# One token tile at a time across the boundary between two layers, partly in plain fp32, and adaLN column sums without GpSimd

## The chip, the core and the metric

The kernel runs on one core of a Trainium2 chip. The metric is the device time of one execution in microseconds (us), the median of several runs. TensorE's granted clock has two levels in these traces, 2.4 GHz (shown as 1.00) and 1.2 GHz (shown as 0.50).

## The reference

Two layers, one after the other, on 256 tokens of width 2048. All is fp32. Cut to what matters here:

```
mod = c @ w_ada + b_ada                      # (2048) @ (2048 x 6144)
shift, scale, gate = split(mod, 3)
u    = layer_norm(x) * (1 + scale) + shift
proj = u @ w_in                              # c_q, c_kv, k_rope, g_a, qkv_b, ... merge_logit
... three attention branches (latent, forgetting, stick-breaking), each gated by silu ...
merged = sum over branches of sigmoid(merge_logit) * (y_n @ w_branch[n])
out  = merged @ w_out                        # (256 x 2048) @ (2048 x 2048)
x    = layer_norm(ALPHA * x + gate * out, ln_g, ln_b)
```

The first product of the second layer needs the rows that the first layer's last layer norm gives, normalised once more and modulated. So the boundary between the layers is a chain: output projection, residual, norm over a row, norm again, transpose, modulate, first product.

## The kernel before

**Tiles.** The 256 tokens are two tiles of 128 (`t` = 0, 1); the width is 16 blocks of 128 (`k`). Activations are the stationary operand of TensorE, weights are the moving one, 512 columns in a matmul, summed in a PSUM bank of 128x512.

**Products in three terms.** Each fp32 operand is split into a rounded part `hi` in the format fp32r and a remainder `lo`; a product is hi·hi + hi·lo + lo·hi, three fp32r matmuls of 128x512 into one bank (`Gemm.multiply`, lines 271 to 273). The weights are split as they arrive: `weight_unit` (line 212) loads 2 k-blocks x 1024 columns (1 MB) on the SP queue into one of four `raw` buffers, ScalarE makes `whi` (line 225), VectorE makes `wlo` (line 227); there are four buffers of each. One pair of 128x1024 feeds 12 matmuls (2 token tiles x 2 halves x 3 terms).

**Order of the work.** The tile framework orders the instructions of each engine at build time: of those that its model takes to be ready, the earliest in the program goes first. The order on each engine is then fixed; on the chip an instruction that waits holds back all behind it on its engine. `tc.issue_after(ins)` keeps instructions behind `ins` on its engine.

**adaLN sums.** c @ w_ada is done in thirds (shift, scale, gate), beside other work: a list `background` is worked off, some pieces per weight unit (`credit`), and emptied by `drain_background`. VectorE sums c·w_ada over 16 steps into `ada_acc` (128 x 2048, line 290), so that a sum over the 128 partitions is left. GpSimd does that with a partition_all_reduce of 128x2048 (line 317). For shift and scale VectorE then masks the result with the identity (line 329) and reduces it (line 332) to 128x16; the gate's row goes to DRAM (line 320). This path serves four of the six thirds: layer 0's gate and all three of layer 1. Layer 0's shift and scale are made by `ada_pieces` (line 549).

**The boundary.** Layer 0's output projection runs as two products of 1024 columns (`cc` = 0, 1; line 849), each for both token tiles; the second finishes its banks one after the other (`stagger`). `evac_out` (lines 844 to 847) multiplies a bank by the gate, adds the residual and takes bn_stats: three VectorE instructions per bank. When all banks of a tile are there, lines 859 to 870 normalise its row: an aggregate, rsqrt (nine instructions on 128x1, lines 179 to 187), four 128x512 instructions on line 864 and four on line 868. `normalise_row` (lines 350 to 359) squares the row on ScalarE for the variance, takes another rsqrt and writes `xn`, half on VectorE and half on ScalarE. `modulate` (line 361) transposes two k-blocks of both tiles on TensorE (line 365) and makes `uhi` and `ulo`. Then `first` (line 526), the first product of layer 1 (columns 0 to 1023 of w_in, all 16 k-blocks, both tiles), can begin.

Of the kernel before, what the change touches and what calls it, by code (L numbers as in the profile page):

```python
# [9 lines left out]
F32 = mybir.dt.float32  # L10
# [27 lines left out]
C0 = GB0 + BW  # L38
M0 = C0 + 4 * BW


@with_exitstack
def trunk(
# [81 lines left out]
    nc.gpsimd.memset(m_mla[0:64, P + 64:], NEG)  # L125
    rst = const.tile([P, 3 * P], F32, name="rst")
# [85 lines left out]
    def weight_unit(parts, width, u):  # L212
        raw = wpool.tile([P, 2, CH], F32, tag="raw", name="raw")
        o = 0
        for src, c0, w in parts:
# [4 lines left out]
            o += w  # L220
        pairs = []
        for j in range(2):
            hi = wpool.tile([P, CH], F32R, tag="whi", name="whi")
            lo = wpool.tile([P, CH], F32R, tag="wlo", name="wlo")
            nc.scalar.activation(hi[:, :width], raw[:, j, :width], AF.Copy)  # L225
            with tc.issue_after(state["first"].ins) if "first" in state else nullcontext():
                state["dve"] = nc.vector.tensor_tensor(  # L227
                    out=lo[:, :width], in0=raw[:, j, :width], in1=hi[:, :width].bitcast(F32), op=ALU.subtract
                )
            pairs.append((hi, lo))  # L230
        return pairs

    class Gemm:
# [9 lines left out]
        def unit(self, u):  # L243
            if u == 0:
                for t in range(NT):
                    for h in range(len(self.cuts)):
                        self.banks[t, h] = acc_tile()
            pairs = weight_unit(self.parts, self.width, u)
# [16 lines left out]
        def multiply(self, t, h, k, pair):  # L265
# [4 lines left out]
            ah, al = ahi[:, k, t * P:(t + 1) * P], alo[:, k, t * P:(t + 1) * P]  # L270
            nc.tensor.matmul(ps, ah, hi[:, o:o + w], start=k == 0, stop=False)  # L271
            nc.tensor.matmul(ps, ah, lo[:, o:o + w], start=False, stop=False)  # L272
            nc.tensor.matmul(ps, al, hi[:, o:o + w], start=False, stop=k == self.nk - 1)  # L273
# [7 lines left out]
    def gemm(*args):  # L281
        Gemm(*args).run()
# [18 lines left out]

    mods = [const.tile([P, 2, KT], F32, name=f"mod{l}") for l in range(DEPTH)]
    gates = {}

    def queue_ada(l, third, tag="ada"):
# [16 lines left out]
        def done():  # L322
# [583 lines left out]
```

## Time and profile before

| what | value |
|---|---|
| median of 3 runs | 2176.76 us (2174.96 to 2179.47) |
| the profiled execution | 2176.92 us, its span 2175.2 us |
| mean granted clock of TensorE | 0.985 |
| TensorE matmul busy | 2071.8 us, 95% of the span |
| VectorE busy | 1455.5 us, 67% |
| ScalarE busy | 984.4 us, 45% |
| GpSimd busy | 66.5 us, 3% |
| moved by DMA | 483 MB, 222 GB/s |

The span runs from the first to the last instruction; the execution's own time is 1.7 us longer. A busy share is an average over stages. Matmuls are pipelined and their ends are modelled, so what a matmul costs in a stream is read from the distance between starts. One fp32 matmul that isn't fp32r is recorded as two.

### The profile page before, as it was taken

What the parts mean: (1) busy time and instruction counts of PE and PEld (TensorE: products, weight loads), DVE (VectorE), ACT (ScalarE), POOL (GpSimd) and SP (SyncE); (2) the same over time, 40 slices, a digit from 0 to 9 for tenths busy, and PEclk for the clock granted to TensorE, in tenths of its full rate; (3) what the DMA queues carried; (4) which work ended last, traced back from release to release, by engine and by line L of the source; (5) the groups of instructions that cost most, each with busy time, mean ns of one, the idle gap of its engine ahead of it and who ended that gap; (6) DMA issues with size and microseconds to landing.
All of it is one profiled execution on the core that took longest, in us unless ns stands there. A gap on an engine that the chain in (4) does not pass through costs nothing. (4 is left out here: it accounts for less than half of the span.)

```text
span 2175.2 us, 24840 instructions
## 1 busy us (share of the span) xinstructions
PE 2071.8 (95%) x9606; PEld 1700.4 (78%) x9606; DVE 1455.5 (67%) x1951; ACT 984.4 (45%) x1257; POOL 66.5 (3%) x79
## 2 busy tenths in 40 slices
PE   4999999999999999999969999999989999999996
PEld 2877888887788878787848888888868888878885
DVE  6898855777558777888587755555575544466466
ACT  4535644444453445634354644444434444464441
POOL 0000000002000020002000000000020000000000
PEclk8999999999999999999979999999999999999998
DMA  8996635787548867786635646666654555556652
GB/s 312 344 332 242 194 117 183 281 309 270 195 145 313 316 232 261 292 320 222 201 135 169 232 136 232 232 230 225 233 178 161 191 193 188 194 180 209 190 200 97
DMA packets 138133, 483.14 MB, mean 222 GB/s; under 512 B 14736, under 2 KB 18976, under 8 KB 127520
## 3 DMA queue, kind: packets, MB, share of 16 engines
q1 hardware_dynamic: 133296, 464.69, 61.6%
q0 software_dynamic: 2432, 16.81, 2.0%
q8 instruction: 75, 1.23, 0.2%
q10 hardware_dynamic: 2288, 0.07, 0.1%
q14 instruction: 42, 0.34, 0.0%
HBM read 477.31 MB, written 4.23 MB: 221 GB/s over the span
## 5 line engine op out<-in xcount | busy, mean ns | idle before, releaser
L227 DVE TENSOR_TENSOR wlo<-raw,whi 128x1024 fp32r<-128x1024 f32 (+2 forms) x648 | 813.0, 1261 | 559.6 <-ACT whi L225 559.3
L225 ACT ACTIVATE whi<-raw 128x1024 fp32r<-128x1024 f32 (+2 forms) x648 | 677.5, 1051 | 826.9 <-PE acc L273 784.1
L272 PE MATMUL acc<-wlo,uhi 128*128 128x512 f32 (+1 forms) x1856 | 733.3, 395 | 11.4 <-DVE wlo L227 11.3
L271 PE MATMUL acc<-whi,uhi 128*128 128x512 f32 (+1 forms) x1856 | 728.4, 394 | 4.0 <-ACT whi L225 3.9
L273 PE MATMUL acc<-whi,ulo 128*128 128x512 f32 (+1 forms) x1856 | 727.9, 392 | 0.0
L272 PEld LDWEIGHTS acc<-wlo,uhi 128*128 128x128 f32 x1856 | 351.5, 189 | 80.3 <-DVE wlo L227 13.3
L271 PEld LDWEIGHTS acc<-whi,uhi 128*128 128x128 f32 x1856 | 350.0, 189 | 73.0 <-ACT whi L225 4.3
L273 PEld LDWEIGHTS acc<-whi,ulo 128*128 128x128 f32 x1856 | 351.1, 189 | 67.1
L272 PE MATMUL acc<-wlo,yhi 128*128 128x512 f32 x384 | 149.5, 389 | 2.0 <-DVE wlo L227 2.0
L273 PE MATMUL acc<-whi,ylo 128*128 128x512 f32 x384 | 149.4, 389 | 0.0
L271 PE MATMUL acc<-whi,yhi 128*128 128x512 f32 x384 | 149.4, 389 | 0.0
L290 DVE SCALAR_TENSOR_TENSOR ada_acc<-raw_ada,c_sb,ada_acc 128x2048 f32<-128x2048 f32 x60 | 140.7, 2345 | 0.1
L271 PE MATMUL acc<-whi,mhi 128*128 128x512 f32 x256 | 99.7, 391 | 2.0 <-ACT mhi L191 2.0
L273 PE MATMUL acc<-whi,mlo 128*128 128x512 f32 x256 | 100.5, 392 | 0.0
L272 PE MATMUL acc<-wlo,mhi 128*128 128x512 f32 x256 | 100.0, 391 | 0.0
L317 POOL PARTITION_ALL_REDUCE ada_acc<-ada_acc x4 | 49.9, 12472 | 1248.7 <-DVE ada_acc L290 736.9
L272 PEld LDWEIGHTS acc<-wlo,yhi 128*128 128x128 f32 x384 | 72.1, 188 | 17.5 <-DVE wlo L227 2.5
L273 PEld LDWEIGHTS acc<-whi,ylo 128*128 128x128 f32 x384 | 72.1, 188 | 14.9
L271 PEld LDWEIGHTS acc<-whi,yhi 128*128 128x128 f32 x384 | 72.1, 188 | 14.9
L610 PE MATMUL acc<-wlo,uhi 128*128 128x512 f32 (+1 forms) x192 | 73.6, 386 | 6.4 <-DVE wlo L601 6.4
L609 PE MATMUL acc<-whi,uhi 128*128 128x512 f32 (+1 forms) x192 | 72.1, 384 | 3.7 <-DVE sum_b L615 2.2
L600 ACT ACTIVATE whi<-raw_g 128x1024 fp32r<-128x1024 f32 (+1 forms) x48 | 46.3, 1002 | 59.1 <-DMA raw_g<-in_w_in_dram 53.9
(232 smaller groups left out, 1790.1 us busy)
## 6 DMA issues: line engine op xcount, KB each, us to landing
raw<-in_w_in_dram SPq DMA_DIRECT2D x224, 1024.0 KB, 5.0
raw_ada<-in_w_ada_dram SPq DMA_DIRECT2D x64, 1024.0 KB, 4.8
raw<-in_w_branch_dram SPq DMA_DIRECT2D x48, 1024.0 KB, 5.6
raw_s<-in_w_ada_dram SPq DMA_DIRECT2D x64, 512.0 KB, 5.0
raw<-in_w_out_dram SPq DMA_DIRECT2D x32, 1024.0 KB, 5.5
raw_g<-in_w_in_dram SPq DMA_DIRECT2D x16, 1024.0 KB, 5.8
raw<-in_w_in_dram SPq DMA_DIRECT2D x8, 832.0 KB, 4.4
raw<-in_w_uq_dram SPq DMA_DIRECT2D x8, 768.0 KB, 4.8
```

Of the source, the lines that this page charges most:

```text
L225: nc.scalar.activation(hi[:, :width], raw[:, j, :width], AF.Copy)
L227: state["dve"] = nc.vector.tensor_tensor(out=lo[:, :width], in0=raw[:, j, :width], in1=hi[:, :width].bitcast(F32), op=ALU.subtract)
L271: nc.tensor.matmul(ps, ah, hi[:, o:o + w], start=k == 0, stop=False)
L272: nc.tensor.matmul(ps, ah, lo[:, o:o + w], start=False, stop=False)
L273: nc.tensor.matmul(ps, al, hi[:, o:o + w], start=False, stop=k == self.nk - 1)
L290: nc.vector.scalar_tensor_tensor(out=acc, in0=raw, scalar=col, in1=acc, op0=ALU.mult, op1=ALU.add)
L317: nc.gpsimd.partition_all_reduce(acc, acc, P, bass_isa.ReduceOp.add)
L600: nc.scalar.activation(hi, raw[:, 2 * j:2 * j + 2, :w], AF.Copy)
L609: nc.tensor.matmul(ps, ah, hi, start=j == 0, stop=False)
L610: nc.tensor.matmul(ps, ah, lo, start=False, stop=False)
```

## The change

It touches three things.

1. **adaLN sums.** The partition_all_reduce is gone. `fold` lets VectorE transpose the 128x2048 sums in blocks of 32x32 and reduce them to 128x64; `done` adds the four groups of 32 partitions with a small matmul against `sel32` and adds the bias in four instructions. The gate's row is transposed and sent to DRAM on ScalarE's queue with its bias in it, so the load and the add of `bg` before the output projection go.
2. **Layer 0's output projection, last 1024 columns.** Columns 1024 to 1535 for both tiles; then columns 1536 to 2047 for tile 0 in three terms, then for tile 1 in plain fp32 (`m_last` by the unsplit weights `held`). Each tile's norms stand in the program right behind its columns.
3. **Layer 1's first product.** Its first 8 k-blocks (`PLAIN`) run in plain fp32, tile 0 and then tile 1 (`start_tile`), from unsplit weights; the other 8 in three terms as before. `hi` and `lo` of the first 8 blocks are still made, for the products that follow. Transposes ahead of a split now go by one token tile and four k-blocks.

```diff
-        def total():
-            acc = ada["acc"]
-            nc.gpsimd.partition_all_reduce(acc, acc, P, bass_isa.ReduceOp.add)
-            if third == 2:
-                gates[l] = dram.tile([1, D], F32, name=f"gate{l}")
-                nc.gpsimd.dma_start(out=gates[l], in_=acc[:1])
+        def fold():
+            acc = ada["acc"]
+            turned = wpool.tile([P, 2, CH], F32, tag="raw", name="turned").rearrange("p j n -> p (j n)")
+            part = tmp.tile([P, SEQ], F32, tag="um", name="part", bufs=2)[:, :D // 32]
+            with tc.issue_after(state["dve"].ins):
+                nc.vector.transpose(turned, acc)
+                nc.vector.tensor_reduce(
+                    out=part, in_=turned.rearrange("p (b j) -> p b j", j=32), axis=mybir.AxisListType.X, op=ALU.add)
+            ada["part"] = part
         def done():
-            acc = ada["acc"]
-            with tc.issue_after(state["dve"].ins):
-                diagonal(l, third, acc)
+            ps = att_tile()
+            nc.tensor.matmul(ps[:, :D // 32], sel32, ada["part"], start=True, stop=True)
+            sums = gsum if third == 2 else mods[l][:, third]
+            for j in range(4):
+                q = slice(32 * j, 32 * j + 32)
+                nc.vector.tensor_tensor(out=sums[q], in0=ps[q, j:D // 32:4], in1=bT[l][q, third], op=ALU.add)
             if third == 2:
+                nc.tensor.transpose(ps[:KT, 2 * P:3 * P], gsum, ident)
+                rows = tmp.tile([P, SEQ], F32, tag="um", name="rows", bufs=2)[:KT, :P]
+                nc.vector.tensor_copy(out=rows, in_=ps[:KT, 2 * P:3 * P])
+                gates[l] = dram.tile([1, D], F32, name=f"gate{l}")
+                nc.scalar.dma_start(out=gates[l].rearrange("o (k p) -> (o k) p", p=P), in_=rows)
-        background.append(total)
-        if third < 2:
-            background.extend([lambda: None, lambda: None, done])
+        background.append(fold)
+        background.extend([lambda: None, done])
...
+    def modulated(l, xt_n, k0, um):
+        ps = att_tile().rearrange("p (k s) -> p k s", k=4)
+        for j in range(4):
+            nc.tensor.transpose(ps[:, j], xt_n[:, (k0 + j) * P:(k0 + j + 1) * P], ident)
+        for j in range(4):
+            k = k0 + j
+            nc.scalar.activation(um[:, j], ps[:, j], AF.Identity, bias=sh[:, k:k + 1], scale=sc[:, k:k + 1])
+    def split_act(um, hi, lo):
+        nc.scalar.activation(hi, um, AF.Copy)
+        nc.vector.tensor_tensor(out=lo, in0=um, in1=hi.bitcast(F32), op=ALU.subtract)
...
-            for u in range(KT // 2):
-                if u == 1:
-                    state["first"] = state["xn"]
-                first.unit(u)
+            for u in range(PLAIN // 2, KT // 2):
+                first.unit(u, ahead.pop(u, None))
+                if u == PLAIN // 2:
+                    for t in range(NT):
+                        for k0 in range(0, PLAIN, 4):
+                            split_act(um[:, t, k0:k0 + 4], uhi[t][:, k0:k0 + 4], ulo[t][:, k0:k0 + 4])
...
-        bg = big.tile([P, D], F32, tag="g", name="bg")
-        nc.gpsimd.dma_start(out=bg, in_=b_ada[l:l + 1, 2 * D:].broadcast_to([P, D]))
-        nc.vector.tensor_tensor(out=gate, in0=gate, in1=bg, op=ALU.add)
...
+        def next_rows(t, sums):
+            nc.gpsimd.dma_start(out=x_next[:, t], in_=xt[:, t])
+            nc.vector.tensor_scalar(shift, sums[:, 0:1], -1.0 / 512, None, op0=ALU.mult)
+            for i in range(4):
+                nc.scalar.activation(xn[t][:, s], xt[:, t, s], AF.Square, bias=shift, accum_out=sq[:, i:i + 1])
...
+            rs = rsqrt(var, LN_EPS)
...
+                if i % 2 == 0:
+                    last_dve = nc.vector.tensor_scalar(
+                        xn[t][:, s], xt[:, t, s], mean, rs, op0=ALU.subtract, op1=ALU.mult)
+                else:
+                    last_act = nc.scalar.activation(xn[t][:, s], xt[:, t, s], AF.Identity, bias=nm, scale=rs)
...
+        held = []
+        for q, tag in enumerate(("yhi", "ylo", "sig", "ada")):
+            held.append(quad_load(big.tile([P, 4, 512], F32, tag=tag, name="held"), w_out[l], q, 3 * 512))
+        bank = [acc_tile() for _ in range(NT)]
+        for q in range(4):
+            pairs = half_pairs(quad_load(wpool.tile([P, 4, 512], F32, tag="raw", name="raw_o"), w_out[l], q, CH))
+            for j, (hi, lo) in enumerate(pairs):
+                for t in range(NT):
+                    three(bank[t], mhi[t][:, 4 * q + j], mlo[t][:, 4 * q + j], hi, lo, 4 * q + j)
+        for t in range(NT):
+            evac_out(t, 0, bank[t])
+        bank = [acc_tile() for _ in range(NT)]
+        for q in range(4):
+            for j, (hi, lo) in enumerate(half_pairs(held[q])):
+                three(bank[0], mhi[0][:, 4 * q + j], mlo[0][:, 4 * q + j], hi, lo, 4 * q + j)
+        evac_out(0, 1, bank[0])
+        sums = post_norm(0)
+        for k in range(KT):
+            nc.tensor.matmul(bank[1], m_last[:, k], held[k // 4][:, k % 4], start=k == 0, stop=k == KT - 1)
+        next_rows(0, sums)
+        evac_out(1, 1, bank[1])
+        raws = [weight_load(parts, u) for u in range(PLAIN // 2)]
+        ahead = {PLAIN // 2: weight_load(parts, PLAIN // 2, big.tile([P, 2, CH], F32, tag="ada", name="raw_ahead"))}
+        def start_tile(t):
+            for k0 in range(0, PLAIN, 4):
+                modulated(l + 1, xn[t], k0, um[:, t, k0:k0 + 4])
+            for k in range(PLAIN):
+                for h in range(2):
+                    first.plain(t, h, k, um[:, t, k], raws[k // 2][:, k % 2])
+        start_tile(0)
+        sums = post_norm(1)
+        state["after"] = [i.ins for i in next_rows(1, sums)]
+        start_tile(1)
+        for t in range(NT):
+            for k0 in range(PLAIN, KT, 4):
+                modulate(l + 1, xn, uhi, ulo, k0, t)
```

`three` is the former three matmuls, `post_norm` the former norm of one tile, `half_pairs` splits a load of 4 k-blocks x 512 columns, and `state["after"]` keeps the split of weights behind the norms of tile 1.

## Rows read from the trace of the kernel before

**Rows 1.** Waits of TensorE over the span: engine, line, waited for: us in total, times, longest.
```profile
PE att L365 <- DVE xn L356: 20.8, 2, 18.6
PE acc L272 <- DVE wlo L227: 13.4, 4, 6.5
```
**Rows 2.** Stretches: us, busy us (x count) of PE, PEld, DVE, ACT, POOL, clock, DMA, GB/s.
```profile
798.40:801.80 3.40, 3.40 (x9) 2.64 (x8) 2.09 (x2) 0.60 (x1) 0.36 (x1) 0.50 0.92 353
...
1586.00:1590.00 4.00, 4.00 (x10) 3.13 (x11) 4.00 (x5) 0.21 (x1) 2.58 (x3) 0.50 0.21 36
1057.80:1101.40 43.60, 43.60 (x192) 35.61 (x191) 28.10 (x36) 15.98 (x16) 0.00 (x0) 1.00 0.54 183
1101.40:1120.00 18.60, 0.13 (x1) 0.00 (x0) 18.28 (x63) 5.98 (x6) 1.07 (x2) 0.61 0.37 140
1120.00:1129.50 9.50, 7.13 (x20) 5.27 (x21) 7.87 (x21) 6.23 (x12) 0.00 (x0) 0.50 0.43 156
1129.50:1173.50 44.00, 44.00 (x207) 36.21 (x206) 27.38 (x49) 25.21 (x37) 0.00 (x0) 1.00 0.45 144
20.20:24.50 4.30, 4.30 (x11) 0.84 (x10) 3.60 (x13) 4.08 (x5) 0.00 (x0) 1.00 1.05 387
```
**Rows 3.** TensorE in order of time, those that waited: start, us, instruction [idle before].
```profile
797.14 0.50 PE L272 MATMUL acc<-wlo,uhi 128*128 128x512 f32 x1 [2.04 <-DVE wlo L227]
...
1585.93 0.79 PE L272 MATMUL acc<-wlo,uhi 128*128 128x512 f32 x1 [6.47 <-DVE wlo L227]
```
**Rows 4.** GpSimd in order of time: the last of four on line 317.
```profile
1575.68 11.87 POOL L317 PARTITION_ALL_REDUCE ada_acc<-ada_acc  x1 [457.31 <-DVE ada_acc L290]
```
**Rows 5.** VectorE in order of time, around line 317 and around lines 329 to 332.
```profile
787.84 12.65 DVE L227 TENSOR_TENSOR wlo<-raw,whi 128x1024 fp32r<-128x1024 f32 x4 [0.82 <-ACT whi L225]
...
1577.69 8.19 DVE L227 TENSOR_TENSOR wlo<-raw,whi 128x1024 fp32r<-128x1024 f32 x1
...
820.13 2.28 DVE L329 TENSOR_TENSOR ada_acc<-ada_acc,ident 128x2048 f32<-128x2048 f32 x1
...
823.47 2.28 DVE L332 TENSOR_REDUCE mod<-ada_acc 128x16 f32<-128x2048 f32 x1
```
**Rows 6.** Line 227 by itself: ns shortest/median/longest, first and last start.
```profile
L227 DVE TENSOR_TENSOR wlo<-raw,whi x648: 947/1226/9996, 47.1 to 2148.1; 128x1024 fp32r<-128x1024 f32 x154, 128x768 fp32r<-128x768 f32 x4, 128x840 fp32r<-128x840 f32 x4
```
**Rows 7.** Plain fp32: weight loads ahead of two passes (128x512) of line 568.
```profile
22.41 0.08 PEld L568 LDWEIGHTS acc<-raw_s,c_sb 128*1 128x1 f32 x1 [0.34 <-issue]
22.84 0.08 PEld L568 LDWEIGHTS acc<-raw_s,c_sb 128*1 128x1 f32 x1 [0.35 <-DMA raw_s<-in_w_ada_dram]
```
**Rows 8.** TensorE in order of time: plain fp32 with 128 stationary columns; transposes.
```profile
278.02 0.60 PE L457 MATMUL att<-kT,qT 128*128 128x256 f32 x2
278.46 0.59 PE L457 MATMUL att<-peT 128*128 128x256 f32 x2
...
1009.14 1.04 PE L466 MATMUL att<-ident,merged 128*128 128x128 f32 x8
```
**Rows 9.** Groups on VectorE, 1093 to 1124: count | busy us, mean ns | idle before.
```profile
L864 DVE SCALAR_TENSOR_TENSOR xt<-xt,mv,lg 128x512 f32<-128x512 f32 x8 | 5.9, 743 | 0.0
L868 DVE SCALAR_TENSOR_TENSOR xt<-xt,rq_y,lb 128x512 f32<-128x512 f32 x8 | 5.5, 749 | 0.0
...
L844 DVE TENSOR_TENSOR gt<-acc,gate 128x512 f32<-128x512 f32 x4 | 2.7, 685 | 1.2 <-PE acc L273 1.2
...
L186 DVE SCALAR_TENSOR_TENSOR rq_w<-rq_y,rq_a 128x1 f32<-128x1 f32 x12 | 2.6, 216 | 0.2
```
**Rows 10.** Groups on ScalarE over the span, each shape for itself.
```profile
L225 ACT ACTIVATE whi<-raw 128x1024 fp32r<-128x1024 f32 x616 | 649.6, 1060 | 807.4 <-PE acc L273 768.1 <-DVE merged L805 11.1 <-issue 10.7
...
L191 ACT ACTIVATE mhi<-att 128x512 fp32r<-128x512 f32 x16 | 9.3, 594 | 7.1 <-PE att L466 7.0
...
L359 ACT ACTIVATE xn<-xt,nm,rq_y 128x512 f32<-128x512 f32 x8 | 6.1, 804 | 3.9 <-DVE nm L352 3.9
L191 ACT ACTIVATE cqh<-att,qg 128x128 fp32r<-128x128 f32 x16 | 5.8, 363 | 5.8 <-DVE cql L192 3.5 <-PE att L504 2.2
```

More of the change, by code (lines that the diff above doesn't have):

```diff
@@ L5 @@
 import concourse.tile as tile
-from concourse import bass_isa, mybir
+from concourse import mybir
 from concourse.masks import make_identity
@@ L220, in weight_unit, with split_weights, weight_pairs @@
             o += w
+        return raw
+    def split_weights(raw, hi, lo):
+        with ExitStack() as order:
+            for ins in state.get("after", ()):
+                order.enter_context(tc.issue_after(ins))
+            nc.scalar.activation(hi, raw, AF.Copy)
+            state["dve"] = nc.vector.tensor_tensor(out=lo, in0=raw, in1=hi.bitcast(F32), op=ALU.subtract)
+    def weight_pairs(raw, width):
         pairs = []
@@ L224, in weight_unit, with half_pairs, quad_load, three @@
             lo = wpool.tile([P, CH], F32R, tag="wlo", name="wlo")
[L225 to L229, printed above, removed]
+            split_weights(raw[:, j, :width], hi[:, :width], lo[:, :width])
             pairs.append((hi, lo))
         return pairs
+    def half_pairs(raw):
+        pairs = []
+        for j in range(2):
+            hi = wpool.tile([P, 2, 512], F32R, tag="whi", name="whi")
+            lo = wpool.tile([P, 2, 512], F32R, tag="wlo", name="wlo")
+            split_weights(raw[:, 2 * j:2 * j + 2], hi, lo)
+            pairs += [(hi[:, 0], lo[:, 0]), (hi[:, 1], lo[:, 1])]
+        return pairs
+    def quad_load(raw, src, q, c0):
+        nc.sync.dma_start(
+            out=raw, in_=src[q * 512:(q + 1) * 512, c0:c0 + 512].rearrange("(k p) n -> p k n", p=P))
+        return raw
+    def three(ps, ah, al, hi, lo, k, n=KT):
+        nc.tensor.matmul(ps, ah, hi, start=k == 0, stop=False)
+        nc.tensor.matmul(ps, ah, lo, start=False, stop=False)
+        nc.tensor.matmul(ps, al, hi, start=False, stop=k == n - 1)
     class Gemm:
@@ L241, in __init__, with open, unit @@
             self.banks = {}
-        def unit(self, u):
+        def open(self):
+            for t in range(NT):
+                for h in range(len(self.cuts)):
+                    self.banks[t, h] = acc_tile()
+        def unit(self, u, raw=None):
             if u == 0:
[L245 to L248, printed above, removed]
+                self.open()
+            pairs = weight_pairs(raw or weight_load(self.parts, u), self.width)
             if self.stagger and u >= self.nk // 2 - 2:
@@ L851, in trunk, with post_norm @@
                 drain_background()
[L852 to L858 removed]
+        def post_norm(t):
             mv = moments(sts[t])
@@ new lines, in trunk @@
+        first.open()
+        def start_tile(t):
[8 more added lines that the diff above has]
+        start_tile(1)
+        for t in range(NT):
+            for k0 in range(PLAIN, KT, 4):
+                modulate(l + 1, xn, uhi, ulo, k0, t)
```

166 lines of the change are left out of this document (99 added, 67 removed).

## The prediction

> **What bounds the kernel now.** The page gives TensorE 95% of the span, so the end moves only where TensorE waits, runs at the lower clock, or gets other work. I read the waits of TensorE first [rows 1]: 20.8 us in two waits for `xn` of the layer boundary, 13.4 us in four waits for `wlo`. The reader is to see that both are of few, long waits, and that the change touches both.
>
> The four waits for `wlo` have one cause. Line 317 runs on GpSimd four times, some 12 us each [rows 4]; in each, one `wlo` of VectorE that takes 1.23 us by its median takes up to 10.0 us [rows 6]: four of them took 12.65 us instead of 4 x 1.23 = 4.9, and one alone 8.19 [rows 5]. TensorE eats up its split weights and waits: 6.47 us in the last place, 13.4 - 6.5 = 6.9 us in the other three [rows 1, 3]. After two of the four the granted clock fell: 3.4 us at 0.50 from 798.4, and from 1586 to 1590 [rows 2].
>
> The boundary, by stretches [rows 2]: the 192 matmuls of the projection's second half fill 43.6 us, 0.227 us each at clock 1.00. TensorE then does nothing to 1120, is fed poorly and at 0.50 to 1129.5, and is full and at 1.00 from there until the first product's 192 matmuls are through at 1173.5. From 1101.4 to 1173.5 are 72.1 us. Needed are 192 x 0.227 = 43.6 and 32 transposes at 0.11 (eight take 1.04 with about 0.27 of latency [rows 8]) = 3.5. So the boundary loses 72.1 - 47.1 = 25.0 us. VectorE is busy 18.28 of the 18.6 empty us [rows 2]: the norms of both tiles in a row are what ends last.
>
> **The change, part by part.**
>
> *Price of plain fp32.* A pass over 512 columns starts 0.43 us after the one before at clock 1.00 [rows 2, 7]; with 128 stationary columns two passes of 256 start 278.46 - 278.02 = 0.44 apart [rows 8], the same 0.43 per 512 columns, so the weight load stays hidden. Two passes make one product: 0.86 us. It replaces three fp32r matmuls, 0.68. The new passes are 48: 16 for the last columns of tile 1, 16 for each tile of layer 1's first half. 48 x (0.86 - 0.68) = +8.7 us. From below the price could be that of two fp32r matmuls, 0.45 (48 x -0.23 = -11 us); from above that of clock 0.50 throughout, 1.72 (+50 us). I take 0.86, from the rows of the same operation. The Trainium skill (FP8 and Floating Point Precision, TensorE Precision Notes) says true fp32 takes four passes through the array; four at 0.227 would be 0.91 and the term +11 us, an estimate. The trace has two records, each as long as two such passes; the measured start distance decides, 0.86.
>
> *The chain of a tile, now alone.* From the last matmul of tile 0's columns: about 0.3 to VectorE; `evac_out`, three instructions at 0.69 by line 844 [rows 9], 2.1; an aggregate 0.3; four of line 864 at 0.74 with the rsqrt (nine small ones, the longest 0.22) between them, 4.3; four of line 868, 2.8. Then the new statistics: the last Square of 512 with its accumulator, 0.9 (from 0.80 of line 359, [rows 10]); four small ones 0.6 and a rsqrt that nothing hides, 1.8; the last scalar 0.2. That is 13.3. ScalarE then does its two quarters of `xn` (1.6) before the first modulating ACTIVATE of 128 columns (0.36), so the first plain matmul of layer 1 can start at 13.3 + 1.6 + 0.4 = 15.3. TensorE meanwhile has tile 1's last columns, 16 x 0.86 = 13.8. Left open: 15.3 - 13.8 = 1.5 us. Tile 1's chain starts when these end and again takes 15.3, that is to 13.8 + 15.3 = 29.1; tile 0's plain products run from 15.3 to 29.1 plus 0.5 of transposes. Nothing is open there by this count; I put 0.5 for hand-overs.
>
> *Split weights.* While tile 0 alone is multiplied a pair of `whi`, `wlo` lasts 6 x 0.227 = 1.36 us, not 2.72. VectorE needs 1.23 for each and has also two `evac_out` (4.1) from the columns before; eight pairs and these are 13.9 us, against 10.9 of matmuls. Three pairs can be ready ahead, so 5 x 1.23 + 4.1 = 10.3 fits as a sum. But those three last 3 x 1.36 = 4.1, and the fourth comes at worst behind both `evac_out`, at 4.1 + 1.23 = 5.3; I put 1.3. (If TensorE's order lets it take tile 1's plain products there, the gap returns behind them.) Before the other 8 blocks ScalarE has 24 ACTIVATEs of 0.36, four splits of 0.59 and two `whi` of 1.06 [rows 10], 13.1 us, beside the 13.8 of tile 1's plain products: close, 1.0 for it. The split of the first 8 blocks (4 x 0.59) lies beside the 21.8 us that follow.
>
> *DMAs.* The queue of SP gets the same 8 MB of w_out and the same w_in, in other shapes. `held` is loaded in the 43 us of the first half, 4 MB more there; the three `big` buffers that branch 2 used and `ada` are free by then. The four `raw` buffers with layer 1's weights are held until both tiles' plain products have read them; unit 4 has a buffer of its own and unit 5 has some 10 us from the release of the first. I cost this at nothing; without that cover one 1 MB load would show, 5.7 us at the 184 GB/s of that half [rows 2].
>
> Boundary: -25.0 + 8.7 + 1.3 + 1.5 + 0.5 + 1.0 = -12.0 us.
>
> *adaLN sums.* The three places inside gemms lose their waits: -6.9, and the low clock behind 797: half of 3.4, -1.7. In place of the stall stand two VectorE instructions, `transpose` and reduce. The reduce over 2048 is 2.28 [rows 5]; a VectorE transpose is in no row. Nearest from above and of its size is line 329, 2.28; from further up the stalled `wlo`, 10.0; from below a 512-column instruction four times less, 0.69. I take 2.3, so 4.6 together. The same 4.6 already stood between weights at lines 329 and 332 [rows 5], and no wait of TensorE is there; the stall of 7.7 shows what slack there was, some 5.5. So 0 for three of the four. The Trainium skill (Vector Engine (DVE) Microarchitecture Reference, 3.8) has that transpose at one element per cycle and lane; 2048 at its 0.96 GHz would be 2.1, an estimate, and no run here shows it yet.
>
> The fourth place is the drain of layer 1: both steps stand right behind the last sums and, by program order, ahead of the `wlo` that started at 1577.69. That one would end at 1577.69 + 4.6 + 1.23 = 1583.5; TensorE wants it at 1585.93 - 6.47 = 1579.5. So 4.0 of 6.5 us of wait stay; the low clock (2 us by 1586 to 1590 at half) I halve. -2.5 - 1.0 = -3.5. Bounds: 0 to -8.5. Sum: -6.9 - 1.7 - 3.5 = -12.1 us.
>
> *What I cost at nothing.* `done`'s matmul of 64 columns, five small VectorE instructions and one transpose, far less than 1 us in place, four times; the gate's store on ScalarE's queue, read hundreds of us later; `bg`'s add, beside matmuls; `sel32` at the start, six small instructions while VectorE waits for data; layer 0's modulation, the same columns in another grouping; the transposes before each projection by tile, where tile 1's first block comes behind tile 0's four groups of 0.59 on ScalarE [rows 10], covered by tile 0's own matmuls on its first four blocks (4 x 6 x 0.227 = 5.4). Each within 1 us either way.
>
> Sum: 2176.9 (profiled execution, its span and 1.7 around it) - 12.0 - 12.1 = 2152.8. The median before is 2176.8, so nothing is to be corrected: **2153 us**.
>
> **Rivals.**
>
> *A, the boundary gives nothing.* The order fixed on VectorE puts tile 1's `evac_out`, which waits for the end of the plain products, ahead of tile 0's last small steps, or some of the chain stands twice. For it: my count has 15.3 against 13.8, a near tie, and VectorE's order is fixed by a model whose durations I don't know. Against: the program has tile 0's norms ahead of it. Two gaps of 6 us instead of 1.5 and 0.5, with a fall of the clock: 2165.
>
> *B, the sums give nothing.* The transpose costs like the stalled `wlo`, 8 to 10 us, and VectorE falls behind as before. For it: no row of a transpose. Against: all fp32 VectorE rows go by elements. 2153 + 12 = 2165. A and B together: 2177, no change.
>
> *C, slower: plain passes at 1.2 GHz.* Place: the 48 products. TensorE at 0.50 took 0.40 to 0.43 per fp32r matmul [rows 2]; a plain product would take 1.72. If all do: +41, 2194. It decides from 24.1 / 0.86 = 28 of 48 on. For it: the clock fell at 798.4 right after a wait of only 2.04 us [rows 2, 3], and my gaps are 1.5. Against: from 20.2 to 24.5 plain passes alone ran at 1.00 [rows 2], and after gaps it came back in 3 to 10 us. One fall costs 2 to 4 us, which the range holds. The Trainium skill (TensorE: Matmul & The Clock Gate, Why this matters for your kernels) warns in the same direction: an idle gap between bursts of matmuls brings the half rate back.
>
> *D, more than forecast.* The small gaps are all filled and the drain's `wlo` goes ahead of the fold: -25.0 + 8.7 = -16.3 and -13.4 - 3.7 = -17.1, less some hand-overs: 2146.
>
> **How the numbers follow.** Forecast 0.48 (by itself 2148 to 2159); A 0.16; B 0.10; D 0.16; A and B 0.05; C 0.05. The range 2145 to 2168 holds the forecast, A, B and D, 0.90 of the chance, less what spills over its ends. 0.2% of 2177 is 4.4 us, about what a measurement here can tell from no change. Faster: 0.48 + 0.16 + 0.10 + 0.16 = 0.90; same 0.05; slower 0.05.
>
> **What would show it.** No VectorE instruction on a `wlo` of more than some 2 us; no wait of TensorE for `wlo` near the first three sums, 0 to 4 us at the drain. Two records per plain product with starts 0.43 apart at clock 1.00; 0.85 would be C. One wait of 1 to 2 us for `um` before tile 0's plain products, almost none before tile 1's; waits of 5 and more there would be A. A fold of 4 to 5 us; 10 would be B. From the start of the projection's last 1024 columns to the end of the first product 115.7 us before, some 104 after. The forecast is wrong if the time is above 2165, where one of the two halves gave nothing.

## The result: 2166.1 us, half of the gain that was forecast

| | before | after |
|---|---|---|
| median | 2177.23 us (4 runs, 2174.96 to 2179.47) | 2166.10 us (4 runs, 2164.55 to 2166.61) |
| ratio to before | | 0.9948, 95% interval 0.9930 to 0.9965 |
| span of the profiled execution | 2175.2 us | 2164.2 us |
| mean granted clock | 0.985 | 0.989 |

It is faster by 11 us; forecast were 24. The time lies in the range (2145 to 2168), not in the forecast's own (2148 to 2159), and above the 2165 us that the prediction named as the mark of being wrong. It is within 1.1 us of the time given to rivals A and B, though neither of them happened as described. So the time alone can't say what went wrong; the trace has to.

TensorE's waits after, those in the places that the change touches. Of [rows 1], the wait for `wlo` in the three-term products is gone and the 20.8 us for `xn` have become 4.8; a new one of 5.4 us for `part` has come.

```profile
PE att L373 <- DVE part L367: 5.4, 1, 5.4
PE att L414 <- DVE xn L971: 4.8, 1, 4.8
...
PE acc L675 <- ACT whi L667: 1.6, 1, 1.6
...
PE att L414 <- ACT um L418: 1.2, 1, 1.2
```

Stretches of the kernel after, columns as in [rows 2]: layer 0's first group products, the place of the stall at 790 to 798, the boundary in six parts, and the drain of layer 1.

```profile
215.00:222.00 7.00, 4.46 (x23) 3.34 (x22) 6.83 (x28) 4.18 (x9) 0.00 (x0) 1.00 0.00 0
222.00:226.00 4.00, 4.00 (x14) 3.50 (x13) 3.30 (x10) 1.70 (x3) 0.00 (x0) 0.57 0.78 262
790.00:806.00 16.00, 16.00 (x73) 13.23 (x72) 11.68 (x8) 6.66 (x8) 0.00 (x0) 1.00 0.76 265
1052.93:1086.48 33.55, 33.55 (x148) 27.40 (x146) 24.19 (x28) 14.27 (x14) 0.00 (x0) 1.00 0.31 111
1086.48:1099.35 12.87, 12.87 (x31) 5.50 (x29) 9.93 (x32) 2.93 (x8) 0.54 (x1) 1.00 0.16 66
1099.35:1106.07 6.72, 1.90 (x10) 1.67 (x9) 6.53 (x24) 2.13 (x4) 0.00 (x0) 0.76 0.55 187
1106.07:1122.81 16.74, 16.63 (x41) 7.58 (x41) 11.54 (x39) 10.18 (x23) 0.53 (x1) 0.89 0.15 63
1122.81:1139.71 16.90, 15.53 (x44) 7.35 (x44) 3.67 (x5) 7.86 (x18) 0.61 (x2) 1.00 0.67 226
1139.71:1162.11 22.40, 22.40 (x100) 18.47 (x101) 12.80 (x27) 13.98 (x25) 0.00 (x0) 1.00 0.49 154
1570.50:1577.40 6.90, 6.36 (x22) 5.17 (x23) 5.49 (x12) 2.00 (x2) 0.52 (x1) 0.51 0.53 165
```

Each stretch of the boundary but the hole begins with a matmul: the fp32r ones of the last columns (with one plain product early among them), 15 plain products for tile 1's columns, then a hole of 6.7 us (with eight transposes at its end), tile 0's plain products with a stay at the lower clock among them, tile 1's, and the rest of the first product. From 1052.93 to 1162.11 are 109.2 us; before, from 1057.64 to 1173.47, 115.8. So the boundary gave 6.65 of the 12.0 forecast.

The new operations: VectorE's groups over the span, and then by itself the line of the plain products (ns shortest/median/longest) and that of `wlo`, which is now never longer than 1.23 us, where [rows 6] has 10.0.

```profile
L366 DVE STREAM_TRANSPOSE turned<-ada_acc 128x2048 f32<-128x2048 f32 x4 | 9.2, 2302 | 0.0
L367 DVE TENSOR_REDUCE part<-turned 128x64 f32<-128x2048 f32 x4 | 9.1, 2283 | 0.1
```
```profile
L317 PE MATMUL acc<-raw,um x64: 592/592/1126, 1106.1 to 1136.2; 128*128 128x512 f32 x64
...
L236 DVE TENSOR_TENSOR wlo<-raw,whi x622: 946/1226/1229, 46.3 to 2137.1; 128x1024 fp32r<-128x1024 f32 x148, 128x768 fp32r<-128x768 f32 x4, 128x840 fp32r<-128x840 f32 x4
```

To see where the time went, I took the start of the same TensorE instruction in two traces, along the span. The table has the difference to the kernel before, in us, for this kernel and for the experiments below but evac_late (place in the time of before; negative is earlier; the last line is the end). The difference between two lines is what the place between them gave. Each column is one execution, and its end can lie some 2 us off the median: the profiled ones of sums_only and boundary_only took 2171.92 and 2176.87 us, 2.0 and 2.1 above their medians.

```
before    after  sums   boundary shift  credit done   copies half   before  all    before
                 only   only     early  up     late   late   cover  credit  three  again
  213.0    1.87   0.58   3.53    2.41   4.09   1.11  -0.69   2.12    1.24  -0.59   0.49
  223.0    3.50   3.38   5.18    4.04   5.69   2.64   0.94   3.61    2.74   1.03   1.86
  432.3    3.45   3.32   5.03    3.90   5.63   2.56   0.85   3.56    2.63   0.91   1.73
  567.2    0.74   0.59   4.99    1.22   2.94  -0.13  -1.87   0.86    4.24  -1.81   3.32
  765.5    0.14   0.35   4.80    1.09   1.77  -1.74  -3.45   1.02    4.23  -2.77   2.87
  856.0   -3.55  -3.34   3.24   -2.58  -1.93  -5.45  -7.14  -2.68    2.66  -6.46   1.31
 1009.1   -5.61  -5.41   3.27   -4.60  -3.96  -7.47  -9.18  -4.71    2.73  -8.49   1.36
 1174.6  -11.46  -5.59   0.40  -14.86 -10.02 -13.38 -16.24 -10.81    2.47 -18.70   1.25
 1490.5  -11.38  -5.56   0.46  -14.80 -10.61 -13.31 -16.10 -10.73    9.11 -19.27   1.28
 1776.0  -11.20  -5.17  -0.29  -14.77 -20.59 -12.16 -16.82 -10.88    0.10 -28.14   0.49
 2175.2  -11.01  -5.29  -0.03  -14.57 -20.42 -11.98 -16.58 -10.70    0.09 -27.93   0.51
```

For the kernel after: +1.9 at the start, +1.6 at 222 us, -2.7, -3.7 and -2.1 at the three places of the old stall, -0.6 between them, -5.85 from 1009 to 1174 (of which +0.9 ahead of the projection's last columns and -6.7 behind), +0.2 in the drain of layer 1, +0.2 behind it.

### The profile page after: what moved, and what is told of

Read it like the earlier page. It is cut to its first block, busy times and chain, and to the rows that moved or that the text cites. A ratio compares the mean times of both kernels' runs of the same rounds, so it can differ in the third digit from the quotient of the medians.

```text
span 2164.2 us, 24761 instructions
## 1 busy us (share of the span) xinstructions
PE 2083.5 (96%) x9568; PEld 1694.0 (78%) x9568; DVE 1419.8 (66%) x1951; ACT 985.2 (46%) x1289; POOL 14.3 (1%) x71
## 3 DMA queue, kind: packets, MB, share of 16 engines
q8 instruction: 75, 1.23, 0.2%
## 5 line engine op out<-in xcount | busy, mean ns | idle before, releaser
L236 DVE TENSOR_TENSOR wlo<-raw,whi 128x1024 fp32r<-128x1024 f32 (+2 forms) x622 | 751.0, 1212 | 556.2 <-ACT whi L235 555.4
L235 ACT ACTIVATE whi<-raw 128x1024 fp32r<-128x1024 f32 (+2 forms) x622 | 650.4, 1050 | 770.6 <-PE acc L266 719.0
L265 PE MATMUL acc<-wlo,uhi 128*128 128x512 f32 (+1 forms) x1824 | 719.1, 394 | 0.0
L264 PE MATMUL acc<-whi,uhi 128*128 128x512 f32 (+1 forms) x1824 | 714.1, 394 | 3.8 <-ACT whi L235 3.5
L266 PE MATMUL acc<-whi,ulo 128*128 128x512 f32 (+1 forms) x1824 | 714.4, 392 | 0.0
L264 PEld LDWEIGHTS acc<-whi,uhi 128*128 128x128 f32 x1824 | 343.6, 189 | 71.1 <-ACT whi L235 4.0
L265 PEld LDWEIGHTS acc<-wlo,uhi 128*128 128x128 f32 x1824 | 344.2, 189 | 66.1 <-DVE wlo L236 0.3
L266 PEld LDWEIGHTS acc<-whi,ulo 128*128 128x128 f32 x1824 | 344.1, 189 | 66.0
L264 PE MATMUL acc<-whi,mhi 128*128 128x512 f32 x240 | 93.8, 392 | 2.1 <-ACT mhi L198 2.0
L266 PE MATMUL acc<-whi,mlo 128*128 128x512 f32 x240 | 94.0, 392 | 0.0
L676 PE MATMUL acc<-wlo,uhi 128*128 128x512 f32 (+1 forms) x192 | 74.4, 390 | 6.5 <-DVE wlo L668 6.3
L675 PE MATMUL acc<-whi,uhi 128*128 128x512 f32 (+1 forms) x192 | 72.6, 387 | 5.3 <-DVE sum_b L681 2.2
L677 PE MATMUL acc<-whi,ulo 128*128 128x512 f32 (+1 forms) x192 | 72.8, 383 | 0.0
```

The source lines that it names most:

```text
L235: nc.scalar.activation(hi, raw, AF.Copy)
L236: state["dve"] = nc.vector.tensor_tensor(out=lo, in0=raw, in1=hi.bitcast(F32), op=ALU.subtract)
L264: nc.tensor.matmul(ps, ah, hi, start=k == 0, stop=False)
L265: nc.tensor.matmul(ps, ah, lo, start=False, stop=False)
L266: nc.tensor.matmul(ps, al, hi, start=False, stop=k == n - 1)
L675: nc.tensor.matmul(ps, ah, hi, start=j == 0, stop=False)
```

## The experiments

**Either part alone.** The two kernels take the change apart: the new sums put into the kernel before, and the kernel after with the old sums put back.

```diff
 # sums_only: the kernel before, with
-            nc.gpsimd.partition_all_reduce(acc, acc, P, bass_isa.ReduceOp.add)
+                nc.vector.transpose(turned, acc)
+                nc.vector.tensor_reduce(out=part, ...)
...
 # boundary_only: the kernel after, with
-        background.append(fold)
+        background.append(total)
...
+        bg = big.tile([P, D], F32, tag="g" if l == DEPTH - 1 else "sig", name="bg")
...
```

> Only the adaLN sums are changed against the kernel before (transpose and reduce on VectorE in place of line 317 on GpSimd and the masked sums); the layer boundary stays as it was. Theory: the sums bring what the trace after shows at the first three places, 8.5 to 9 us, and nothing in the drain of layer 1; 2177 - 9 = 2168 us, ratio 0.996. Nothing is lost at the start, since the modulation of layer 0 keeps its order here: at 226 us of the span the start stands within 1 us of the kernel before, not 3.5 later. Rival: the late start (+2.0 by 71 us, +3.5 by 226 us) belongs to this part (the six instructions for sel32, say); then 2171 to 2172 us and the same shift at 226 us.

> Only the boundary and the regrouping that goes with it (modulation and transposes by token tile) are changed; the adaLN sums are the kernel before's (GpSimd, masked sums). Theory: -6.6 us from the end of the projection's first half to the end of layer 1's first product, +3.5 at the start of layer 0, +0.9 before the projection, and the four waits for wlo are back: about 2175 us, ratio 0.999. Rival: the two parts are not independent and the boundary brings the forecast 12 us without the other part: 2165 to 2169 us.

Measured: 2169.94 us (ratio 0.9965, 0.9953 to 0.9978) and 2174.75 us (0.9992, 0.9983 to 1.0000). The sums give 2.7, 3.7 and 2.1 us at the first three places, as in the kernel after, and nothing in the drain. They do not bring the +1.9 at the start (0.6 at 213 us); the boundary's part does (3.5 there, part of it there by 38 us already). But the step at 222 us stands in both, which neither theory had. By the medians the two parts give 6.9 and 2.1 us, 9.0 of the 11.1. The boundary alone gives 2.9 us from 1009 to 1174, less than the 5.9 in the kernel after. The traces show where that went: between 1025 and 1035 us boundary_only loses 3.8 us, a wait of 1.9 for a `wlo` at 1031 and the lower clock behind it; from there to 1174 it gives 7.0, about as much as the kernel after. boundary_only, VectorE ahead of that `wlo`, and the stretch:

```profile
1022.47 2.29 DVE L894 TENSOR_TENSOR gate<-gate,bg 128x2048 f32<-128x2048 f32 x1 [1.84 <-DMA bg<-in_b_ada_dram]
```
```profile
1030.00:1036.00 6.00, 4.46 (x13) 3.54 (x14) 5.33 (x7) 1.06 (x1) 0.00 (x0) 0.72 1.02 390
```

That `wlo` starts at 1030.27, behind the two masked sums of 2.28 and 2.27 us and the add of `bg` ahead of them. The kernel before has the same masked sums there and no such wait; the add comes there by this experiment's own edit, since `m_last` takes the buffer `g` and `bg` must load into `sig`, which comes free later. Both go with the new sums. So the 3.8 us belong to the mixture of old sums and new boundary, and not to either part; no run takes the add away by itself.

**The hole before tile 0's plain products.** VectorE of the kernel after in order of time (start, us, instruction, idle before), and ScalarE beside it:

```profile
1086.68 0.69 DVE L917 TENSOR_TENSOR gt<-acc,gate 128x512 f32<-128x512 f32 x1 [2.92 <-PE acc L266]
...
1095.91 0.15 DVE L950 TENSOR_SCALAR shift<-sums 128x1 f32<-128x1 f32 x1
...
1099.10 0.16 DVE L962 TENSOR_REDUCE var<-sq 128x1 f32<-128x4 f32 x1 [2.29 <-ACT xn L954]
...
1099.48 0.15 DVE L186 TENSOR_SCALAR rq_a<-var 128x1 f32<-128x1 f32 x1
...
1100.38 0.68 DVE L917 TENSOR_TENSOR gt<-acc,gate 128x512 f32<-128x512 f32 x1
1100.98 0.21 DVE L193 SCALAR_TENSOR_TENSOR rq_w<-rq_y,rq_a 128x1 f32<-128x1 f32 x1
...
1103.58 0.15 DVE L967 SCALAR_TENSOR_TENSOR nm<-mean,rq_y 128x1 f32<-128x1 f32 x1
```
```profile
1096.14 0.72 ACT L954 ACTIVATE xn<-xt,shift 128x512 f32<-128x512 f32 x1 [13.86 <-DVE shift L950]
...
1103.83 1.52 ACT L974 ACTIVATE xn<-xt,nm,rq_y 128x512 f32<-128x512 f32 x2 [4.76 <-DVE nm L967]
```

Two things make the chain late. `shift`, which needs only the first quarter's sum, stands behind all four quarters, so ScalarE, which has nothing else to do, starts its four Squares at 1096.14 (the first quarter's sum is there at 1093.97), and `var` waits 2.29 us for them. And tile 1's `evac_out` (from line 917 on) is put between the small steps of tile 0's rsqrt: from `rq_a` to `nm` 4.1 us. shift_early moves `shift` alone, and VectorE's order then comes out without the second as well; evac_late takes away the second alone:

```diff
 # shift_early
+                if skew and i == 0:
+                    shift = small.tile([P, 1], F32, tag="shift", name="shift")
+                    shifts[t] = shift
+                    nc.vector.tensor_scalar(shift, sums[:, 0:1], -1.0 / 512, None, op0=ALU.mult)
...
 # evac_late
-        next_rows(0, sums)
-        evac_out(1, 1, bank[1])
+        done0 = next_rows(0, sums)
+        with tc.issue_after(done0[0].ins):
+            evac_out(1, 1, bank[1])
```

> The changed kernel, with the one small instruction `shift` placed right behind the first of the four quarters that it needs, instead of behind all four; with it VectorE's fixed order has no instruction of tile 1's evac_out between tile 0's small steps. Theory: the wait before tile 0's plain products (6.7 us after the last product of tile 1's columns) is the serial chain of tile 0; the four Squares then run beside the quarters (-2.1) and the rsqrt takes 1.8 instead of 3.35 (-1.5), so the wait falls to about 3 us; if the granted clock then does not fall to 0.50 behind it, -1.8 more. 2166 - 3.6 to 5.4 = 2161 to 2162.5 us. Rival: the time comes back at tile 1, whose evac_out now stands later, as a wait of the same size before tile 1's plain products: 2166 us.

> The changed kernel, with tile 1's evac_out held behind tile 0's last instruction of the norm on VectorE; `shift` stays where it is. Theory: only the interleaving goes, so the rsqrt of tile 0 takes 1.8 instead of 3.35 us and the wait before tile 0's plain products is about 5.2 instead of 6.7 us; 2164.5 us, or 2163 if the clock does not fall behind it. Rival: tile 1's chain, later by its evac_out (2 us), gives the time back before tile 1's plain products: 2166 us or a little more.

Measured: 2161.85 us (0.9929, 0.9916 to 0.9943) and 2164.83 us (0.9940, 0.9928 to 0.9953). shift_early's rows, VectorE in order of time and then the hole, tile 0's plain products, the step to tile 1 and tile 1's; last, evac_late's hole:

```profile
1087.69 0.69 DVE L917 TENSOR_TENSOR gt<-acc,gate 128x512 f32<-128x512 f32 x1 [2.93 <-PE acc L266]
...
1095.56 0.15 DVE L947 TENSOR_SCALAR shift<-sums 128x1 f32<-128x1 f32 x1
...
1098.76 0.16 DVE L967 TENSOR_REDUCE var<-sq 128x1 f32<-128x4 f32 x1 [0.88 <-ACT xn L959]
...
1099.14 0.15 DVE L186 TENSOR_SCALAR rq_a<-var 128x1 f32<-128x1 f32 x1
...
1101.05 0.16 DVE L972 SCALAR_TENSOR_TENSOR nm<-mean,rq_y 128x1 f32<-128x1 f32 x1
```
```profile
1100.36:1103.22 2.86, 1.27 (x9) 0.84 (x9) 2.69 (x9) 1.92 (x4) 0.00 (x0) 1.00 0.74 216
1103.22:1117.06 13.84, 13.84 (x33) 6.08 (x33) 12.28 (x45) 6.85 (x18) 0.53 (x1) 1.00 0.30 123
1117.06:1119.42 2.36, 1.03 (x9) 0.79 (x8) 0.68 (x2) 2.36 (x5) 0.00 (x0) 1.00 0.00 0
1119.42:1133.26 13.84, 13.84 (x32) 6.14 (x33) 5.65 (x6) 6.37 (x12) 0.00 (x0) 1.00 0.60 199
```
```profile
1099.31:1103.78 4.47, 1.93 (x9) 1.67 (x9) 4.05 (x16) 2.13 (x4) 0.00 (x0) 0.78 0.82 275
```

In shift_early `shift` came behind the second quarter, and `var` starts 11.1 us behind the start of `evac_out` instead of 12.4. From `rq_a` to `nm` are now 1.9 us instead of 4.1, the hole is 2.86 instead of 6.72, and the granted clock stays at 1.00 behind it. Of the 3.9 us, 1.3 came back at tile 1, whose chain now starts later: a wait of 1.3 us for `um`, a third of what its rival said. From 1009 to 1174 it gives 10.3 us instead of 5.9, the clock included. In evac_late the hole is 4.47, so the interleaving alone is worth 2.2 us of it and the later Squares the most of the other 1.6. It gives 8.5 us from 1009 to 1174; then it lost 1.8 in the drain, which it doesn't touch, so its median is not set against shift_early's.

**What the plain products buy.**

```diff
-PLAIN = 8
+PLAIN = 4
```

> shift_early with 4 instead of 8 blocks of layer 1's first product in plain fp32: 16 plain products fewer, 48 fp32r matmuls more. Theory (plain products are bought for the time they fill): tile 0's plain products then take 6.9 instead of 13.8 us, and tile 1's chain, which begins when the projection's last columns end and takes some 18 to 19 us to the first plain product of tile 1, no longer has enough beside it: a wait of 7 to 9 us between the two tiles, the same start of tile 1's plain products, 10.9 us of fp32r matmuls instead of 6.9 of plain ones behind it: +4 us, and 1.5 to 3.4 more if the granted clock falls behind the wait: 2166 to 2169. Rival (plain products are only dearer work): 16 x (0.86 - 0.68) = 2.9 us less, 2159.

Measured on top of shift_early: 2166.58 us (0.9949, 0.9935 to 0.9963), 4.7 us above it; from 1009 to 1174 it loses 4.2. The theory holds, with a shorter wait between the tiles than it had (6.2 us, where 7 to 9 stood). TensorE waited in the boundary, half_cover:

```profile
PE att L414 <- DVE xn L976: 7.4, 2, 6.2
```

The longest, 6.2 us, stands between the two tiles: with half the plain products there is too little beside tile 1's chain. So their price isn't waste; at 8 blocks they pay with 13.8 us of TensorE's time for a chain that would be waited for.

**The drain of layer 1.** VectorE of the kernel after, in order of time:

```profile
1556.99 7.12 DVE L334 SCALAR_TENSOR_TENSOR ada_acc<-raw_ada,c_sb,ada_acc 128x2048 f32<-128x2048 f32 x3
1564.03 1.87 DVE L434 SCALAR_TENSOR_TENSOR g<-th,acc 128x512 f32<-128x512 f32 x3
1565.82 2.30 DVE L366 STREAM_TRANSPOSE turned<-ada_acc 128x2048 f32<-128x2048 f32 x1
1568.05 0.65 DVE L434 SCALAR_TENSOR_TENSOR g<-th,acc 128x512 f32<-128x512 f32 x1
1568.62 2.27 DVE L367 TENSOR_REDUCE part<-turned 128x64 f32<-128x2048 f32 x1
```

Three pieces of the sums that the drain hands out at once (7.1 us) stand ahead of transpose and reduce (4.6) with four gate steps (2.5): 14 us in a row, and TensorE stands at the matmul that needs `part`:

```profile
1571.04 0.66 PE L373 MATMUL att<-part,sel 128*128 128x64 f32 x2 [5.44 <-DVE part L367]
```

Before, the same three pieces stood there, but what followed them was GpSimd's, and TensorE had its other products to go on with until the `wlo` of [rows 3]. The first of the two edits hands the pieces out earlier; the second leaves that matmul for later.

```diff
 # credit_up (and before_credit, in the kernel before)
-            credit[1] = 0.2
+            credit[1] = 0.3
...
 # done_late
-    def drain_background():
-        while background:
+    def drain_background(keep=0):
+        while len(background) > keep:
...
-                drain_background()
+                drain_background(1 if l == 1 else 0)
```

> The changed kernel, with the background pieces of layer 1's gate sums handed out at 0.3 a step instead of 0.2, so that all sixteen, transpose, reduce and what follows are through before the drain, and nothing stands in a row there. Theory: the 5.4 us that TensorE waits for `part` in the drain go, and with them the 6.8 us at half the granted clock behind it (3.4): up to 8.8 us, 2157 to 2160. Rival 1: the work on VectorE comes back as waits for wlo in the products before, by 2.3 us or more each: 2162 to 2166. Rival 2: the wait in the drain is set by something else (the forget gate's logarithms on ScalarE, say), and stays: 2166.

> The changed kernel, with the matmul of layer 1's gate sums (and what hangs on it) taken out of the drain and left for a step of the next product; transpose and reduce stay in the drain. It tells the two waits of the forecast apart: TensorE stands in order at the matmul that needs `part` (theory), or it would wait for wlo behind transpose and reduce anyway (the forecast's own 4.0 us). Theory: no wait for `part`, and TensorE has 12 us of other work there, so wlo is late by at most 1 us: 2158 to 2161. Rival, the forecast's step: 4.0 us for wlo and half of the low clock stay: 2162 to 2164.

Measured: 2155.95 us (0.9904, 0.9890 to 0.9917) and 2164.91 us (0.9947, 0.9934 to 0.9959). With the pieces earlier the drain gives 10.0 us where it gave nothing: 5.4 of wait, half of the 6.8 us at the lower clock, and a wait of 1.5 us for `sm` behind. credit_up, TensorE full and at 1.00 through the stretch:

```profile
1550.00:1580.00 30.00, 30.00 (x139) 24.87 (x138) 15.92 (x25) 13.47 (x15) 1.08 (x2) 1.00 0.62 227
```

No wait for `wlo` came in its place. In done_late both sides were wrong: the wait neither goes nor falls on `wlo`, it moves to the next small result that VectorE owes. TensorE's wait, and VectorE's row:

```profile
PE att L806 <- DVE fq L803: 4.9, 1, 4.9
```
```profile
1566.72 2.27 DVE L367 TENSOR_REDUCE part<-turned 128x64 f32<-128x2048 f32 x1
1568.91 0.16 DVE L803 COPY fq<-att 128x16 f32<-128x16 f32 x1
```

`fq`, 0.16 us of work, stands behind the reduce. So the row of work on VectorE is what has to go (credit_up), not one of the instructions that wait for it.

> The kernel before, with nothing changed but the background pieces of layer 1's gate sums handed out at 0.3 a step instead of 0.2. Theory: the 6.5 us of wait and 6.8 us at half clock in the drain are then gone (-9.9), and line 317 on GpSimd stalls a wlo within the products instead, as at the other three places, for 2.0 to 2.5 us: 2176.8 - 7.5 = 2169. Rival: the stall of VectorE beside GpSimd costs as much wherever it stands: 2176, no change.

Measured: 2177.01 us (0.9994, 0.9986 to 1.0003). The rival is right. The drain gives 9.0 us, and 7.2 are lost where the sum now stands, between 1439 and 1490. GpSimd and VectorE there, and TensorE's new wait:

```profile
1483.80 12.70 POOL L317 PARTITION_ALL_REDUCE ada_acc<-ada_acc  x1 [362.74 <-DVE ada_acc L290]
```
```profile
1485.58 9.24 DVE L227 TENSOR_TENSOR wlo<-raw,whi 128x1024 fp32r<-128x1024 f32 x1 [0.82 <-ACT whi L225]
1494.74 1.28 DVE L390 COPY kT<-att 128x512 f32<-128x512 f32 x2
```
```profile
PE att L389 <- DVE kT L390: 5.2, 1, 5.2
```

Line 317 on GpSimd again holds up a `wlo`, 9.24 us. The Trainium skill (SBUF — State Buffer, "SBUF: two separate sides") says that VectorE with two inputs in SBUF and a GpSimd instruction that reads SBUF take a pair of ports in turn, each for a whole instruction. The rows agree in the main: the `wlo` starts 1.8 us behind line 317 and ends 1.7 us ahead of its recorded end, and the profile's spans on GpSimd are rough. So the 10 us of credit_up were not to be had in the kernel before: they need the sums without GpSimd.

**The start.**

```diff
+                while q == 0 and pending:
+                    dst, src = pending.pop(0)
+                    nc.scalar.activation(dst, src, AF.Copy)
...
-                        nc.scalar.activation(sums[t], ps, AF.Copy)
+                        pending.append((sums[t], ps))
```

> The changed kernel, with ScalarE's copies of a group's first sums in layer 0 (line 679) placed behind the two splits of the next group's weights, as ScalarE had them in the kernel before; the modulation stays by token tile. Theory: the 2 us lost by 71 us of the span (a wait of 1.55 us for whi among them) come from that order alone: at 88 us the start stands where the kernel before has it, and the time is 2164. Rival: the loss is the modulation's own work (four ACTIVATEs of 128 columns and one split more per block), or the wait moves to another group; 2166.

> The kernel before, unchanged, profiled a second time. At 222 us of the span the changed kernel and three of its variants (either half of the change alone among them) ran 3 to 4 us at half the granted clock behind a wait of 2.1 us that the kernel before has too, without the fall. Theory: the fall is chance of the execution and shows here as well in some runs; then its 1.5 to 2.8 us belong to no edit. Rival: the kernel before never has it, its clock stays at 1.00 from 222 to 226 us here too, and both parts of the change bring it.

Measured: copies_late 2160.31 us (0.9925, 0.9912 to 0.9939), before_again 2177.43 us. ScalarE in the kernel after, where a copy (line 679) stands ahead of both splits (line 667), and in copies_late, where the splits come first:

```profile
70.04 0.52 ACT L679 ACTIVATE sum_b<-acc 128x420 f32<-128x420 f32 x1 [1.34 <-PE acc L677]
70.46 1.99 ACT L667 ACTIVATE whi<-raw_g 128x1024 fp32r<-128x1024 f32 x2
```
```profile
67.95 2.00 ACT L669 ACTIVATE whi<-raw_g 128x1024 fp32r<-128x1024 f32 x2
69.84 0.51 ACT L675 ACTIVATE sum_b<-acc 128x420 f32<-128x420 f32 x1
```

With ScalarE's old order the start stands at -0.7 instead of +1.9 at 213 us and the wait of 1.55 us for `whi` is gone: the edit that I had costed at nothing, layer 0's modulation by token tile, let the fixed order on ScalarE come out another way. Between 60 and 71 us every trace with that order loses 2.6 to 3.1 us (2.6 in the kernel after), and none of the others loses anything. The other half of its 5.8 us lies in places that it doesn't touch (1.0 between 567 and 765, 1.2 in the boundary, where the stay at half clock was shorter, 0.9 in the drain), and I don't put it down to the edit. before_again has a fall of the clock ahead of 222 us that the first profile of the same kernel hasn't:

```profile
215.00:222.00 7.00, 4.46 (x17) 3.29 (x16) 6.53 (x21) 3.24 (x7) 0.00 (x0) 0.81 0.14 35
222.00:226.00 4.00, 4.00 (x19) 3.47 (x19) 3.28 (x9) 2.25 (x5) 0.00 (x0) 0.91 0.52 201
```

It costs 1.4 us there. The fall shows in this trace, in before_credit, whose start is the same as that of the kernel before, and in every trace with a part of the change. So the +1.4 to +2.8 that all columns have at that place are the luck of one execution, the first profile of the kernel before, and not the change.

**All three edits together.**

> The changed kernel with the three edits that each gained by themselves: `shift` early (-4.3 us of the medians), the pieces of the gate sums handed out faster (-10.1) and ScalarE's copies behind the next splits (-5.8, of which some 2.5 stand at the start and the rest in places that it doesn't touch). Theory: they act in three places of TensorE's time and add up, but for the part of copies_late that a shorter stay at half clock in the boundary brought, which shift_early has already: 2166.1 - 4.3 - 10.1 - 3.5 = 2148, 2146 to 2151. Rival: they share waits, and what one takes away another has taken already: 2153 or more.

Measured: 2148.76 us (0.9865, 0.9851 to 0.9878), 17 us below the kernel after and 30 below the one before. They add up as forecast. The waits of the boundary are near what the prediction had in mind, 1.2 us for `xn` before tile 0's plain products and at most 1.3 for `um` before tile 1's, where it had almost none; there is none for `part`.

## Why the prediction was half wrong, step by step

Terms of the sum against the trace after (a transpose at 0.11 is taken off where a stretch holds some):

```
term                                          forecast   measured
loss of before in the boundary                  -25.0      -25.0
plain price, 48 x (0.86 - 0.68)                  +8.7       +8.7
split weights ahead of tile 0's columns          +1.3        0.0
gap before tile 0's plain products               +1.5       +5.8   6.72 - 8 x 0.11
hand-over, tile 0's plain products               +0.5       +2.1   16.74 - 32 x 0.43 - 8 x 0.11
before the other 8 blocks                        +1.0       +2.0   16.90 and 22.40, the same way
boundary                                        -12.0       -6.4   (span to span -6.65)
sums, three places                               -8.6       -8.5
sums, drain of layer 1                           -3.5       +0.2
what I had put at nothing (start, transposes)     0.0       +2.8   1.9 + 0.9
```

Right: the price of a plain product. 32 passes fill 13.84 us at clock 1.00, 0.43 each. The Trainium skill's four passes (FP8 and Floating Point Precision, TensorE Precision Notes) would be 0.91 per product, an estimate; the trace has 0.86. Right: the fold, 2.30 + 2.28 us where 2.3 + 2.3 stood, so rival B is out. The Trainium skill's one element per cycle and lane (Vector Engine (DVE) Microarchitecture Reference, 3.8) gave an estimate of 2.1. Rival C is out too: the clock fell once in the boundary, as [rows 2] let expect, and came back within tile 0's plain products. (The 184 GB/s of the 1 MB load is 183 in its row; nothing hangs on it.)

Wrong, first: "Left open: 15.3 - 13.8 = 1.5 us." The durations were right: from the start of tile 0's `evac_out` at 1086.68 to the end of the last quarter of its norm at 1095.99 are 9.3 us, where 9.5 were counted. What I counted as lying beside each other did not: I took one Square behind the last quarter where four stood, since I hadn't read where the new `shift` is written (3.1 us from that quarter to the end of the last, where 0.9 was counted); and I took a rsqrt at 1.8 us that had another tile's `evac_out` in it (4.1). The two make the 4.3 us between 1.5 and 5.8, to within 0.2. The interleaving is rival A's mechanism, with its place named rightly, but it was one hole of 6.7 us and not two of 6, and the rest of the boundary worked, so A as a whole did not happen. The hand-over of 2.1 us hangs on that hole: at a clock of 0.89 over 16.74 us, 1.8 of it is the lower clock behind the hole, and with shift_early the clock does not fall. Of the 2.0 us before the other 8 blocks, 1.2 are a wait for `um`. shift_early has nearly the forecast's gap: 2.86 - 0.88 = 2.0.

Wrong, second: the drain, -3.5 forecast and +0.2 measured. VectorE came out as counted: its reduce ends at 1570.89 us, 1582.3 in the time of before (this place stands 11.4 earlier), and 1577.69 + 4.6 is 1582.3 too. The step that failed is that the prediction left TensorE its other products until 1579.5 and then a wait of 4.0 for one `wlo`. It did not ask which of TensorE's instructions stand in order behind the result: TensorE stopped at the matmul for `part` at 1565.6, 1577.0 in the time of before, and waited 5.4; without that matmul `fq`, behind the reduce on VectorE, would have held it (done_late). And the lower clock, which I halved to 1.0, cost 3.4. The bound of 0 all but held it, the value did not.

Wrong, third: "Each within 1 us either way" for the regrouping at the start (1.9 at 213 us: 2.6 lost between 60 and 71, 0.7 gained around it) and before the projection (0.9, of which 0.4 is a wait for `mlo` that before has not; the rest is small holes that no run took apart).

Not forecast by anyone: that with three small edits the same change gives 2148.8, where rival D had 2146, though by other ways than D's.

## What to carry to other kernels

Where a chain is meant to be hidden by work that is barely longer, the sum of durations is not enough: read in the code where each small instruction stands, and ask on each in-order engine what is issued between its steps and what stands ahead of it; moving one instruction of 0.15 us ahead was worth 4.3 us here, a good half of the gap by the other order that it led to. When a task moves from an idle engine to one that is busy, see that it does not arrive together with a batch of its own input: handing the pieces out earlier was worth nearly as much as the whole change (10.1 and 11 us). And take a time that equals a rival's for no proof of the rival until the places in the trace agree.

## What the runs showed of the hardware that I had not expected

Around the same wait of 2.1 us for a `wlo`, at 217 to 226 us, the granted clock fell or did not fall in two executions of one and the same kernel, for 1.4 us (from 215 to 222 us 1.00 in the first, which kept it, and 0.81 in the second). Of the thirteen traces twelve have the fall, though the wait is only 2.1 us long. So a comparison of two profiles can hold a step of this kind that belongs to no edit. And the stall of a `wlo` beside line 317 was about as long wherever it stood: 8.2 to 10.0 us in the kernel before, 9.24 in before_credit; moving it brought nothing that the medians show.
